# Cosine-similarity attention on one core: the TensorE warm-up reads the array of ones, and the five engine orders are replaced

## The chip, the core and the metric

The kernel runs on one core of one Trainium2 chip. A core has five engines that work side by side: TensorE (matrix multiplication, "PE" in the profile, with its weight loads as "PEld"), VectorE ("DVE"), ScalarE ("ACT"), GpSimd ("POOL") and SyncE ("SP", here only an issuer of transfers). Each runs its own list of instructions in order, and they wait for one another through semaphores. The metric is the device time of one execution in microseconds (us); shown is the median of several runs.

## The reference

For 8 batches and 12 heads, each with 512 queries, 512 keys and 64 dimensions, in float32:

```python
Q_norm = Q / (np.linalg.norm(Q, axis=-1, keepdims=True) + 1e-10)
K_norm = K / (np.linalg.norm(K, axis=-1, keepdims=True) + 1e-10)
scores = np.einsum('bhqd,bhkd->bhqk', Q_norm, K_norm) / tau
weights = np.exp(scores - np.max(scores, axis=-1, keepdims=True))
weights = weights / (np.sum(weights, axis=-1, keepdims=True) + 1e-10)
return np.einsum('bhqk,bhkd->bhqd', weights, V)
```

tau is 0.1, so the scores lie between -10 and 10.

## The kernel before

The 96 heads are worked in 48 **pairs** (s = 0 to 47). For each pair these operations exist, and the names below are the ones that the rest of the text uses:

- LD(s,0) and LD(s,1) load Q and K of a pair, LV(s) loads V (256 KB each, line 396 and 399). Pair 0 is loaded in four halves by line 393, LD(0,w,h), with w = 0 for Q, 1 for K, and h for the head. ST(s) stores the result. All but the two K halves of pair 0 and one last store are issued by SP, in the order of SP's list.
- SQ(s,...) squares Q and K. In pairs 0 to 3 it is cut in parts that ACT and POOL share (lines 329, 331, 414, 416), later it is one POOL instruction for the pair (line 422).
- SSQ(s,w) sums eight slices of the squares on TensorE (eight matmuls against the identity, line 440), and RED(s,w) on VectorE adds up what is left (line 448). Without SSQ, RED does the whole sum (line 452).
- Pairs 0 and 1 get the reciprocal root of the norm on ACT: LOG and then an exponential, NRMS for pair 0 (lines 337, 339), NEW(1,7) for pair 1 (lines 470, 473). Later groups do it on VectorE in steps NEW(g,0) to NEW(g,8) (lines 481 to 490).
- SCL(s,w) multiplies Q or K by it (lines 342, 521), on VectorE or POOL; CST(0,h) is the like for K of pair 0 (lines 316, 319).
- TR(s,w) are four transposes on TensorE (lines 351, 353, 528), and EVA(s) copies them out of PSUM on VectorE (lines 364, 536).
- SCO(s,c) and, from pair 12 on, SCG(n) are the score matmuls (lines 621, 286); EXP and EXG are the exponentials on ACT that empty the score banks (lines 626, 630, 302, 641). Pair 0 has four exponentials of 512 columns for head 0 and two of 1024 for head 1; then there are groups of 1024 and, from pair 12 on, of 1024 and 1536 columns in turn over five PSUM banks.
- VC(s) casts V on POOL (line 646). PV(s,h,i), four matmuls each (line 658), multiplies the weights with V; a column of ones in V gives the sum of the weights. RCP and NRM on VectorE divide (lines 671, 673).
- One quarter of pair 43 has its exponential on VectorE and POOL instead of ACT (steps X and Y, lines 580 to 588).

Before all this TensorE runs **warm** (line 203): eight matmuls of 512 columns whose result nobody reads. FILL(0) to FILL(9) (line 206) are single matmuls of 64 to 384 columns, also unread, that stand in between in TensorE's list. `warm` waits for the POOL instruction that makes the identity (line 193, out of the array of ones that line 192 writes) and for a VectorE memset of the array `warm_in` (line 207).

The **order** of each engine is written out by hand: `ORDER` holds, for each of the five, the numbers of the operations in the order in which they were added, and line 37 in `schedule` turns them into lists. The waits follow from the operations' needs; nothing is reordered at run time, so an instruction that waits holds up all that stand behind it on its engine, SP's transfers too. The head of the lists, in names (pairs 0 and 1 up to the first group of pair 1):

```
POOL  one eye eps vone SQ(0,1,1) SQ(0,1,0) CST(0,1) SQ(1,1,1) SQ(2,0) SQ(2,1) SQ(3,0) SQ(3,1) VC(0)
ACT   SQ(0,0,0) CST(0,0) SQ(0,0,1) LOG(0,0,0) NRMS(0,0,0) LOG(0,1,1) NRMS(0,1,1) LOG(0,0,1) LOG(0,1,0) NRMS(0,0,1)
      SQ(1,0) NRMS(0,1,0) SQ(1,1) EXP(0,1,0) EXP(0,0,0) LOG(1) NEW(1,7) EXP(0,3,0) EXP(0,2,0) EXP(0,0,1) EXP(0,2,1) EXP(1,0)
PE    warm FILL(9) FILL(4) TR(0,1,0) TR(0,0,0) FILL(3) FILL(2) FILL(0) TR(0,1,1) SCO(0,1,0) SCO(0,3,0) SCO(0,0,0) FILL(1)
      SSQ(1,0) SSQ(1,1) TR(0,0,1) SCO(0,2,0) FILL(6) FILL(5) SSQ(2,0) FILL(7) SCO(0,0,1) SCO(0,1,1) SSQ(2,1)
      TR(1,1) TR(1,0) SCO(0,3,1) SCO(0,2,1) SSQ(3,0) FILL(8) SSQ(3,1) SCO(1,0) PV(0,0,0)
DVE   wz RED(0,0,0) RED(0,1,1) RED(0,0,1) SCL(0,0,0) RED(0,1,0) EVA(0,1,0) EVA(0,0,0) EVA(0,1,1) SCL(0,0,1) RED(1,0) RED(1,1)
SP    LD(0,0,0) LD(0,0,1) LD(1,0) LD(1,1) LD(2,0) LD(2,1) LD(3,0) LD(3,1) LV(0)
```

Of the kernel before, what the change touches and what calls it, by code (L numbers as in the profile page):

```python
# [118 lines left out]
def bass_cosine_similarity_attention_kernel(  # L119
# [8 lines left out]
    BATCH, NHEAD, SEQ, DIM = Q.shape  # L128
    assert SEQ == 512 and DIM == 64 and NHEAD % 2 == 0
    NT = SEQ // 128  # L130
# [6 lines left out]
    def sb(name, shape, dt):  # L137
        return nc.alloc_sbuf_tensor(name, shape, dt)
# [14 lines left out]
    ones = sb("ones", [128, 128], bf16)  # L153
    ident = sb("ident", [128, 128], bf16)
    eps = sb("eps", [128, 1], f32)
    warm_in = sb("warm_in", [128, SEQ], bf16)
# [12 lines left out]
    P = Program(nc)  # L169
# [31 lines left out]
    def warm(e):  # L201
        for k in range(WARM):
            last = e.matmul(out=o_ps[1][:, :], lhsT=ident[:, :], rhs=warm_in[:, :], start=True, stop=True)
        return last

    P.fill = lambda e, n: e.matmul(out=o_ps[1][:, 0:n], lhsT=ident[:, :], rhs=warm_in[:, 0:n], start=True, stop=True)
    P.add("wz", "dve", "sm_dve", -100, [], lambda e: e.memset(warm_in[:, :], 0.0))
    P.add("warm", "pe", "warm", -100, ["eye", "wz"], warm)
# [566 lines left out]
def slack(s, most):  # L775
# [13 lines left out]
    ),  # L789
    "pool": (  # L790
# [6 lines left out]
    ),  # L797
    "dve": (
# [22 lines left out]
    ),  # L821
# [75 lines left out]
```

## Time and profile before

| | us |
|---|---|
| median of 3 runs | 188.52 (188.34 to 188.87) |
| the profiled execution, its own time | 188.81 |
| span of its instructions | 187.0 |
| ACT busy | 180.1 (96%) |
| PE busy | 174.6 (93%) |
| DVE busy | 169.5 (91%) |
| POOL busy | 161.8 (87%) |

The span runs from the first to the last instruction of the profiled execution; 1.8 us of its time lie outside. A row of the timeline reads: start, duration (both us), engine, line, operation, output and inputs, number of instructions merged, and in brackets the idle time before it and what ended that. A busy share says little here, since four engines are near full; what matters is which wait ends last in a stretch.

### The profile page before, as it was taken

What the parts mean: (1) busy time and instruction counts of PE and PEld (TensorE: products, weight loads), DVE (VectorE), ACT (ScalarE), POOL (GpSimd) and SP (SyncE); (2) the same over time, 40 slices, a digit from 0 to 9 for tenths busy, and PEclk for the clock granted to TensorE, in tenths of its full rate; (3) what the DMA queues carried; (4) which work ended last, traced back from release to release, by engine and by line L of the source; (5) the groups of instructions that cost most, each with busy time, mean ns of one, the idle gap of its engine ahead of it and who ended that gap; (6) DMA issues with size and microseconds to landing.
All of it is one profiled execution on the core that took longest, in us unless ns stands there. A gap on an engine that the chain in (4) does not pass through costs nothing.

```text
span 187.0 us, 6660 instructions
## 1 busy us (share of the span) xinstructions
PE 174.6 (93%) x2714; PEld 106.2 (57%) x2714; DVE 169.5 (91%) x552; ACT 180.1 (96%) x186; POOL 161.8 (87%) x150
## 2 busy tenths in 40 slices
PE   6998999999999999999999999999999899899992
PEld 2555666556665556466566565556655465455562
DVE  1799999999999999989999989899999999979663
ACT  5789999999999999999999999999999999999993
POOL 3699999999999999999999999899999796495300
PEclk9999999999999999999999999999999999999999
DMA  5999999999999999998799999994646925001537
GB/s 167 329 354 352 350 349 349 343 377 383 366 317 332 301 380 358 321 376 274 177 368 306 329 382 365 379 370 155 200 135 172 326 68 171 4 0 57 171 110 234
DMA packets 52446, 50.76 MB, mean 271 GB/s; under 512 B 3136, under 2 KB 52416, under 8 KB 52416
## 3 DMA queue, kind: packets, MB, share of 16 engines
q1 hardware_dynamic: 51984, 50.02, 81.6%
q8 instruction: 21, 0.34, 0.8%
q10 hardware_dynamic: 432, 0.33, 0.5%
q14 instruction: 9, 0.07, 0.1%
HBM read 37.75 MB, written 12.58 MB: 269 GB/s over the span
## 4 chain that ended last, share of the span: by engine, by line
ACT 92%; DMA 3%; PE 2%; DVE 1%; issue 0%; SPq 0%
ACT et L302 90%; DMA qk<-in_Q_dram 3%; DVE qn L521 1%; ACT et L630 1%; PE scps L286 1%; SPq L393 0%; ACT et L641 0%; ACT sq L414 0%; PE ops L440 0%; PE scps L621 0%; ACT ob L706 0%; DVE ob L710 0%; PE tps L528 0%; PE ops L689 0%; DVE rd L702 0%
## 5 line engine op out<-in xcount | busy, mean ns | idle before, releaser
L302 ACT ACTIVATE et<-scps 128x1024 bf16<-128x1024 f32 (+1 forms) x159 | 169.0, 1259 | 0.3 <-PE scps L286 0.2
L422 POOL TENSOR_TENSOR sq<-qk 128x1024 bf16<-128x1024 f32 x44 | 83.3, 1908 | 0.0
L286 PE MATMUL scps<-qt 64*128 64x512 bf16 x374 | 74.0, 385 | 6.7 <-ACT et L302 4.6
L658 PEld LDWEIGHTS ops<-vb,et 128*128 128x128 bf16 x1504 | 55.6, 98 | 32.1 <-issue 16.5
L658 PE MATMUL ops<-vb,et 128*128 128x65 bf16 x1504 | 72.0, 194 | 0.3 <-DVE ob L673 0.3
L521 POOL TENSOR_TENSOR qn<-qk,rk 128x512 bf16<-128x512 f32 x38 | 39.8, 1055 | 2.1 <-DVE rk L486 1.9
L673 DVE TENSOR_TENSOR ob<-ops,rd 128x256 f32<-128x256 f32 x94 | 39.0, 417 | 0.8
L528 PE MATMUL tps<-ident,qn 128*128 128x128 bf16 x376 | 33.3, 220 | 0.4 <-DVE ys L481 0.3
L536 DVE COPY qt<-tps 128x1024 bf16<-128x1024 bf16 x47 | 32.1, 682 | 1.5 <-PE tps L528 1.2
L646 POOL TENSOR_SCALAR vb<-vf 128x512 bf16<-128x512 f32 x48 | 30.2, 640 | 3.0 <-DVE et L587 3.0
L528 PEld LDWEIGHTS tps<-ident,qn 128*128 128x128 bf16 x376 | 21.6, 98 | 13.1 <-issue 7.4
L286 PEld LDWEIGHTS scps<-qt 64*128 64x128 bf16 x374 | 16.3, 93 | 22.1 <-ACT et L302 13.8
L521 DVE TENSOR_TENSOR qn<-qk,ops 128x512 bf16<-128x512 f32 x41 | 27.0, 674 | 0.0
L452 DVE TENSOR_REDUCE xn<-sq 128x8 f32<-128x512 bf16 x38 | 25.2, 674 | 0.2
L671 DVE RECIPROCAL rd<-ops 128x4 f32<-128x4 f32 x94 | 16.1, 175 | 5.0 <-PE ops L658 3.7
L440 PE MATMUL ops<-sq,ident 128*128 128x64 bf16 x384 | 19.0, 193 | 0.0
L440 PEld LDWEIGHTS ops<-sq,ident 128*128 128x128 bf16 x384 | 14.3, 98 | 3.9 <-issue 2.4
L521 DVE TENSOR_TENSOR qn<-qk,scps 128x512 bf16<-128x512 f32 x15 | 9.9, 676 | 0.1
L448 DVE TENSOR_REDUCE xn<-ops 128x8 f32<-128x64 f32 x34 | 7.0, 210 | 0.5 <-PE ops L440 0.5
L416 POOL TENSOR_TENSOR sq<-qk 128x512 bf16<-128x512 f32 (+1 forms) x5 | 4.6, 956 | 1.1 <-DMA qk<-in_K_dram 1.0
L452 DVE TENSOR_REDUCE scps<-sq 128x8 f32<-128x512 bf16 x8 | 5.4, 684 | 0.1
L587 POOL TENSOR_TENSOR xz<-xz 128x1024 f32<-128x1024 f32 x1 | 1.9, 1893 | 3.9 <-DVE xz L582 3.9
(73 smaller groups left out, 78.4 us busy)
## 6 DMA issues: line engine op xcount, KB each, us to landing
vf<-in_V_dram SPq DMA_DIRECT2D x48, 256.0 KB, 6.2
qk<-in_Q_dram SPq DMA_DIRECT2D x47, 256.0 KB, 6.4
qk<-in_K_dram SPq DMA_DIRECT2D x47, 256.0 KB, 6.2
out_dram<-ob SPq DMA_DIRECT2D x47, 256.0 KB, 4.6
qk<-in_Q_dram SPq DMA_DIRECT2D x2, 128.0 KB, 2.6
qk<-in_K_dram ACTq DMA_DIRECT2D x2, 128.0 KB, 2.9
out_dram<-ob SPq DMA_DIRECT2D x1, 128.0 KB, 2.2
out_dram<-ob SPq DMA_DIRECT2D x1, 64.0 KB, 1.9
```

The source lines that it names most:

```text
L286: last = e.matmul(out=sc_ps[:, b, :], lhsT=qt[s % R_QT][64 * h : 64 * h + 64, 1, c, :], rhs=qt[s % R_QT][64 * h : 64 * h + 64, 0, :, :], s ...
L302: lambda e: e.activation(out=et_all[:, i : i + len(us), :], in_=sc_ps[:, banks[0] : banks[0] + len(us), :], func=ACT.Exp, scale=math.log(2 ...
L422: lambda e: e.tensor_tensor(out=sqf, in0=data, in1=data, op=ALU.mult))
L440: last = e.matmul(out=o_ps[bank][:, 320:384], lhsT=ident[:, :], rhs=sq[iqs][:, 8 * w : 8 * w + 8, 8 * k : 8 * k + 8], start=(k == 0), stop ...
L452: lambda e, w=w, dst=dst: e.tensor_reduce(out=dst, in_=sq[iqs][:, 8 * w : 8 * w + 8, :], axis=AX.X, op=ALU.add))
L521: lambda e, w=w, r=r: e.tensor_tensor(out=qn[iqn][:, w].rearrange("p t h d -> p h t d"), in0=qk[iq][:, w].rearrange("p h (t d) -> p h t d" ...
L528: last = e.transpose(t_ps[:, w, t, :], qn[iqn][:, w, t].rearrange("p h d -> p (h d)"), ident[:, :])
L536: lambda e: e.tensor_copy(out=qt[iqt][:, :, :, :].rearrange("p w t x -> p (w t x)"), in_=t_ps[:, :, :, :].rearrange("p w t x -> p (w t x)")))
L646: lambda e: e.tensor_scalar(out=vb[:, iq, :, :, 0:DIM].rearrange("p c h d -> p h c d"), in0=vf[iv][:, :, :].rearrange("p h (c d) -> p h c ...
L658: last = e.matmul(out=o_ps[h][:, 65 * t : 65 * t + 65], lhsT=et[iet][:, c, h, 128 * t : 128 * t + 128], rhs=vb[:, iq, c, h, :], start=(c = ...
L671: lambda e, h=h, grid=grid: e.reciprocal(out=rd[io][:, h, :], in_=grid[:, :, DIM]))
L673: lambda e, h=h, grid=grid: e.tensor_tensor(out=ob[io][:, h], in0=grid[:, :, 0:DIM], in1=rd[io][:, h, :].unsqueeze(2).to_broadcast([128, N ...
```

## The change

The array `warm_in` and its VectorE memset go away. `warm` and the FILLs take the array of ones both as the weights and as the moving operand, which repeats its 128 columns four times (64 columns n/64 times for a FILL of n columns); `warm` now waits for the memset of the ones alone. The numbers of columns and of matmuls stay. All five orders are replaced. The operation `wz` is gone from the list, so every number above 5 stands for the operation that had one more before.

```diff
-    warm_in = sb("warm_in", [128, SEQ], bf16)
...
     def warm(e):
         for k in range(WARM):
-            last = e.matmul(out=o_ps[1][:, :], lhsT=ident[:, :], rhs=warm_in[:, :], start=True, stop=True)
+            last = e.matmul(out=o_ps[1][:, :].rearrange("p (k x) -> p k x", k=NT), lhsT=ones[:, :], rhs=ones[:, :].unsqueeze(1).to_broadcast([128, NT, 128]),
+                            start=True, stop=True)
         return last
 
-    P.fill = lambda e, n: e.matmul(out=o_ps[1][:, 0:n], lhsT=ident[:, :], rhs=warm_in[:, 0:n], start=True, stop=True)
-    P.add("wz", "dve", "sm_dve", -100, [], lambda e: e.memset(warm_in[:, :], 0.0))
-    P.add("warm", "pe", "warm", -100, ["eye", "wz"], warm)
+    P.fill = lambda e, n: e.matmul(
+        out=o_ps[1][:, 0:n].rearrange("p (k x) -> p k x", x=64), lhsT=ones[:, :],
+        rhs=ones[:, 0:64].unsqueeze(1).to_broadcast([128, n // 64, 64]), start=True, stop=True)
+    P.add("warm", "pe", "warm", -100, ["one"], warm)
...
     "sp": (
-        "7 8 68 69 107 108 152 153 11 196 197 240 239 70 109 273 316 274 154 315 198 392 349 658 350 469 393 427 502 241 "
+        "6 7 67 68 106 107 152 151 10 195 196 238 239 315 69 272 273 108 348 153 314 349 425 392 391 240 105 426 197 316 "
...
```

The head of the new lists, in names:

```
POOL  one eye eps vone SQ(0,1,0) SQ(0,1,1) CST(0,1) SQ(1,1,1) SQ(2,0) SQ(2,1) SQ(3,1) SQ(3,0) VC(0)
      SQ(4,0) SQ(5,0) VC(1) SCL(3,1) SQ(6,0) VC(3) VC(2) SCL(5,1) SQ(7,0) SQ(8,0) SQ(9,0) VC(4) SCL(6,1)
ACT   SQ(0,0,0) CST(0,0) LOG(0,0,0) SQ(0,0,1) NRMS(0,0,0) LOG(0,1,1) NRMS(0,1,1) LOG(0,0,1) NRMS(0,0,1) LOG(0,1,0)
      SQ(1,0) SQ(1,1) NRMS(0,1,0) EXP(0,0,0) LOG(1) NEW(1,7) EXP(0,3,0) EXP(0,1,0) EXP(0,2,0) EXP(0,0,1) EXP(0,2,1) EXP(1,0)
PE    warm TR(0,1,0) FILL(3) FILL(4) FILL(1) FILL(2) TR(0,0,0) TR(0,1,1) FILL(0) SCO(0,0,0) TR(0,0,1) FILL(9)
      SSQ(1,0) SSQ(1,1) SCO(0,2,0) SCO(0,3,0) SCO(0,1,0) FILL(6) FILL(5) FILL(7) SSQ(2,0) SCO(0,0,1) SCO(0,3,1) SSQ(2,1)
      SCO(0,1,1) TR(1,0) TR(1,1) SCO(0,2,1) FILL(8) SSQ(3,1) SSQ(3,0) SCO(1,0) PV(0,0,0)
DVE   RED(0,0,0) RED(0,1,1) RED(0,0,1) SCL(0,0,0) EVA(0,1,0) RED(0,1,0) EVA(0,0,0) SCL(0,0,1) EVA(0,1,1) RED(1,0) RED(1,1)
SP    LD(0,0,0) LD(0,0,1) LD(1,0) LD(1,1) LD(2,0) LD(2,1) LD(3,1) LD(3,0) LV(0) LD(4,0) LD(4,1) LD(5,0) LD(5,1) LD(7,1)
      LV(1) LD(6,0) LD(6,1) LV(2) LD(8,0) LV(3) LD(7,0) LD(8,1) LD(10,0) LD(9,1) LD(9,0) LV(5) ST(1) LD(10,1) LV(4) LV(7)
```

In the old lists POOL goes on after VC(0) with SQ(4,0) SQ(5,0) VC(1) SCL(3,1) VC(2) SQ(6,0) VC(3) SQ(7,0) SCL(5,1) VC(4) SQ(8,0) SQ(9,0) SCL(6,1), and SP has no store among its first 46 issues. TensorE has SCO(5,1) PV(4,0,0) PV(4,0,1) PV(4,0,2) SCO(5,2) in the old list and one PV(4,0,3) more ahead of SCO(5,2) in the new one. ACT's list from EXP(1,0) to its end is the same in both, and so are the last 23 entries of VectorE's.

144 rows, old and new, of the table ORDER are left out of this document.

## The prediction

> **What bounds the kernel now.** I read the page first, its span and its costliest line, the exponentials.
>
> ```profile
> span 187.0 us, 6660 instructions
> ...
> L302 ACT ACTIVATE et<-scps 128x1024 bf16<-128x1024 f32 (+1 forms) x159 | 169.0, 1259 | 0.3 <-PE scps L286 0.2
> ```
>
> Ahead of all 159 exponentials of line 302 ACT idled 0.3 us in all, and they alone take 169 us. The chain of waits in order of time says where the rest lies:
>
> ```profile
> 13.20 154.88 ACT et L302 x146
> ...
> 168.12 0.62 PE scps L286 x3
> ...
> 182.20 0.73 ACT et L641
> ```
>
> From 13.20, where EXP(1,0) starts, to 182.20 the end is set by ACT alone, but for one wait of a few tenths at 168. Its list from EXP(1,0) on is the same in both versions. So the time is **13.2 us of head, 169 us of ACT at its own pace, and a tail**. A better order can shorten the head and the tail; in the middle it can only lose. That one wait is of pair 43: a group of a single score bank covers too little for the next three, whatever the order; I leave it in.
>
> The head on ACT, from its timeline:
>
> ```profile
> 6.95 0.63 ACT L414 ACTIVATE sq<-qk 128x512 bf16<-128x512 f32 x1 [0.21 <-DMA qk<-in_Q_dram]
> 7.49 0.19 ACT L339 ACTIVATE xs<-ys 128x4 f32<-128x4 f32 x1
> 7.61 0.42 ACT L414 ACTIVATE sq<-qk 128x256 bf16<-128x256 f32 x1
> 7.93 1.25 ACT L630 ACTIVATE et<-scps,xs 128x512 bf16<-128x512 f32 x2
> 9.10 0.31 ACT L470 ACTIVATE ys<-xs,eps 128x16 f32<-128x16 f32 x1
> 9.56 1.25 ACT L630 ACTIVATE et<-scps,xs 128x512 bf16<-128x512 f32 x2
> 10.70 1.02 ACT L626 ACTIVATE et<-scps 128x1024 bf16<-128x1024 f32 x1
> 12.10 1.02 ACT L626 ACTIVATE et<-scps 128x1024 bf16<-128x1024 f32 x1 [0.38 <-PE scps L621]
> 13.20 7.44 ACT L302 ACTIVATE et<-scps 128x1024 bf16<-128x1024 f32 x8
> ```
>
> Two exponentials of 512 columns take 1.14 us from 9.56 to the start of the next, 0.57 each; one of 1024 takes 0.92 (eight in 7.44). ACT thus lost 0.48 us ahead of 12.10 and 0.18 ahead of 13.20. What holds 13.20 is not ACT, but what feeds SCO(1,0):
>
> ```profile
> 7.65 4.72 POOL L416 TENSOR_TENSOR sq<-qk 128x256 bf16<-128x256 f32 x5 [1.03 <-DMA qk<-in_K_dram]
> ```
>
> ```profile
> 12.43 0.41 PE L440 MATMUL ops<-sq,ident 128*128 128x64 bf16 x8
> 12.77 0.39 PE L286 MATMUL scps<-qt 64*128 64x512 bf16 x2
> ```
>
> **POOL's five squares** run without a gap from the landing of pair 1's K (7.6) to 12.37; the sums of the last one stand on TensorE ahead of SCO(1,0) (12.43), which starts at 12.77, ends at 13.16, and EXP(1,0) follows. So the head is set by a load and by POOL. The new orders keep this chain: POOL has the same five squares behind the same load (its last two exchanged), TensorE has both SSQ of pair 3 ahead of SCO(1,0), and SP's first six issues are the same.
>
> **The change part by part.** *The warm-up.*
>
> ```profile
> 0.78 0.20 POOL L192 MEMSET ones<- 128x128 bf16 x1 [0.29 <-POOLq L879]
> 1.06 0.29 POOL L193 TENSOR_SCALAR_AFFINE_SELECT ident<-ones 128x128 bf16<-128x128 bf16 x1
> 1.41 3.60 PE L203 MATMUL ops<-warm_in,ident 128*128 128x512 bf16 x8 [1.41 <-POOL eps L196]
> 5.31 0.64 PE L353 MATMUL ops<-ident,qn 128*64 128x128 bf16 x4
> 6.07 0.47 PE L353 MATMUL tps<-ident,qn 128*64 128x128 bf16 x4
> 6.86 0.39 PE L351 MATMUL ops<-ident,qn 128*128 128x128 bf16 x4
> 7.18 0.82 PE L621 MATMUL scps<-qt 64*128 64x512 bf16 x3
> ```
>
> The ones are there at 0.98, the identity at 1.35: the warm-up starts 0.37 us earlier, near 1.04. The removed memset frees nothing: what follows it on VectorE, RED(0,0,0), waits for ACT's first square. Its eight matmuls took 3.60 us with the last one's drain, so at most 0.45 each, or 0.88 ns a column. How fast a repeated operand is read the profile doesn't show; I take the same, and bound it by nothing below and, above, by twice (the warm-up then ends at 8.2 instead of 4.6), which would delay the first scores by over 1 us. Four transposes took 0.64 us at 5.31, 0.47 at 6.07 and 0.39 at 6.86, and three scores of 512 columns 0.82 at 7.18, where the warm-up had 0.45 for each: TensorE runs at **half clock until about 6.2**, 4.8 us after its first matmul. If the 4.8 us hold, the switch comes at 5.8. As the other end I take a half clock that lasts through the old order's first three scores, to 8.0.
>
> A rule speaks against counting on that: the Trainium skill, "TensorE: Matmul & The Clock Gate", Part 1, says the activity window (an estimate by its figure: 3.4 us) runs freely and doesn't start with the kernel, so that the same kernel has a different number of slow matmuls from run to run. By it the switch could come at any time from 4.5 to 7.9; by the one execution traced, at 5.8. One profile can't decide.
>
> *The head in its new order.* TensorE: warm to about 4.5, TR(0,1,0) (0.5 without its drain), then 1152 columns of FILL (1.0 us at half clock) to about 6.0, TR(0,0,0). That waits for SCL(0,0,0), and VectorE has the same three RED ahead of it:
>
> ```profile
> 5.61 0.41 DVE L342 TENSOR_TENSOR qn<-qk,scps 128x256 bf16<-128x256 f32 x1
> ...
> 8.84 0.22 DVE L448 TENSOR_REDUCE xs<-ops 128x8 f32<-128x64 f32 x1 [0.15 <-PE ops L440]
> ...
> 11.77 0.68 DVE L536 COPY qt<-tps 128x1024 bf16<-128x1024 bf16 x1
> ```
>
> So TR(0,0,0) starts at 6.07 as before, with its copy and TR(0,1,1) behind it SCO(0,0,0) falls near 7.2, where the old order had its first score, and is done at 7.6. On ACT both SQ now stand ahead of NRMS(0,1,0), which before filled the wait at 7.49: SQ(1,1) at 7.61, NRMS at 7.93, EXP(0,0,0) at 8.05. Cost so far 0.12.
>
> LOG(1) is next, one exponential earlier than before. It needs the second RED of pair 1, 8.84 plus 0.22, which hangs on POOL's half square (7.65 plus 0.6) and so on the load: **9.10 again**. ACT waits from 8.67 to 9.10, 0.43 us. Then come NEW(1,7) and, from 9.56 as before, three exponentials of 512 instead of two to 11.27, two of 1024 to 12.19 and 13.11. TensorE's share fits: SCO(0,1,1) needs EXP(0,1,0) done (10.13 plus 0.65) and ends at 11.23; the eight transposes of pair 1 follow to 11.77; SCO(0,2,1) ends at 12.08, before 12.19. EVA(1) moves from 11.77 to 11.80 and is done at 12.48, under the last SSQ, which POOL releases at 12.43 as before. SCO(1,0) goes at 12.77.
>
> Sum for the head: ACT alone could start EXP(1,0) at 13.11, 0.09 earlier; POOL holds it at 13.20. **Gain 0.00**, between 0.09 better and about 0.3 worse: at half clock to 8.0, SSQ(1,1) and LOG(1) come 0.3 late, and 13.11 becomes 13.41. A landing of K earlier than in this execution would gain up to 0.4 more, since LOG(1) now stands behind one exponential where two held it at 9.10.
>
> *The middle.* TensorE and ACT are both near full, and any order may break a feed. The tightest place I found is pair 4's cast of V:
>
> ```profile
> 17.22 1.05 POOL L521 TENSOR_TENSOR qn<-qk,rk 128x512 bf16<-128x512 f32 x1
> ...
> 24.13 0.64 POOL L646 TENSOR_SCALAR vb<-vf 128x512 bf16<-128x512 f32 x1
> 24.71 3.75 POOL L422 TENSOR_TENSOR sq<-qk 128x1024 bf16<-128x1024 f32 x2
> ```
>
> ```profile
> 28.35 0.54 PE L658 MATMUL ops<-vb,et 128*128 128x65 bf16 x12
> ```
>
> VC(4) stood at 24.13, 4 us early. Now SQ(8,0) and SQ(9,0) go first: from 17.22 SCL 1.0, SQ(6,0) 1.86, two casts 1.16, SCL 1.0, three SQ 5.6, so VC(4) at 27.8, done at 28.45. PV(4,0,0), at 28.35 before, starts near 28.55, with four PV (sixteen matmuls at 0.03, 0.5) ahead of SCO(5,2) instead of three: that ends near 29.5, and EXP(5,2) is due near 29.6 (18 steps of 0.91 behind EXP(1,0)). Cost 0, with 0.1 us to spare.
>
> *The tail* has the same last entries on ACT and VectorE: 0.
>
> **Sum.** The profiled execution is 187.0 of span and 1.81 around it, 188.81, 0.29 above the median of 188.52. All terms are zero, so I forecast 188.5 for the median, its own range 188.1 to 189.0 (0.4 for an earlier landing, 0.5 for 0.3 of clock and 0.2 at POOL's edge). I call same what lies within 0.3%, 0.57 us, about what a measurement of this kernel can tell from no change.
>
> **Rivals.** (1) *The clock gains.* If the typical execution before keeps half clock to 8.0 instead of 6.2, the old order suffers: FILL(3), FILL(2), FILL(0), 896 columns, cost 0.4 more (half of 0.88 ns each), the transposes 0.25 a group (0.64 less 0.39), and EXP(0,0,0) stands behind three scores at double length, so that LOG(1) comes some 0.85 later (0.4, 0.25, and 0.2 for the two scores ahead of it); the new order, with one score and few columns there, loses the 0.2 by which 13.41 passes 13.20. That is 0.6 better: 187.9. For it: the runs before spread over 0.53 us. Against it: the profiled execution has the early switch and is yet slower than the median. The skill's rule above makes such runs possible.
>
> (2) *V comes late*, the losing case. SP's new list has ST(1) as its 27th issue, ahead of LD(10,1) and LV(4).
>
> ```profile
> 15.45 4.30 SPq L396 DMA_DIRECT2D qk<-in_K_dram  x5
> ```
>
> ```profile
> 22.19 0.42 DVE L673 TENSOR_TENSOR ob<-ops,rd 128x256 f32<-128x256 f32 x1
> ```
>
> ```profile
> vf<-in_V_dram SPq DMA_DIRECT2D x48, 256.0 KB, 6.2
> ```
>
> The 27th issue falls near 18.3 (the fourth of those five), but ST(1) waits for NRM(1,1), done at 22.61: SP stands for 4.3 us, and LV(4) is issued near 23.8. With 6.2 us to landing it would be there at 30.0, VC(4) done at 30.65, PV(4,0,0) 2.1 us late, all of it a gap on ACT: 190.6. It decides from a landing after 27.8. Against it: the 6.2 us are mostly queue, seven or eight transfers at the 0.86 us of those five, and five of them are gone when SP moves again at 22.6; two or three are left, and ST(1), LD(10,1) and LV(4) follow, five at 0.86. I put its landing near 27, and 189.6 for half the delay.
>
> (3) *The warm-up does not start earlier*, since something other than the identity holds TensorE to 1.4: then the switch stays where it was, and by the sum above the time too, 188.5.
>
> **Chances.** Forecast with (3), 0.60; (1) 0.17, which is also faster by over 0.3%; (2) and the like of it 0.23, slower. The range from 187.8 to 189.7 holds the forecast, (1), and half of (2).
>
> **What would show it.** Warm-up at 1.04, its eight matmuls again in 3.6 us: first step right. LOG(1) at 9.10 behind a wait of 0.4 on VectorE, POOL's squares again from 7.65 to 12.37, EXP(1,0) at 13.20: the head right. EXP(1,0) before 12.9, or the first square of pair 1 before 7.3: head wrong. Idle time of line 302 still near 0.3: the middle right; a wait near 29.5 with POOL's cast as its cause: (2).

## The result

| | median | lowest and highest | executions |
|---|---|---|---|
| before | 188.61 us | 188.34 to 189.14 | 11 |
| after | 190.37 us | 189.09 to 193.27 | 11 |

The ratio after to before is **1.0069, 95% interval 1.0043 to 1.0095**: the changed kernel is slower. The ratios of this document leave out executions more than 1.5% above the fastest of their kernel: here four of 191.97 to 193.27 us, whose mean granted clock was 0.991 (with them the two medians stand at 1.0093), and below two of twelve with the warm-up alone (192.89 and 193.25), three of six with the old head and the new middle (192.97, 193.44, 218.23) and one of six with only ST(34) moved (215.22). The profiled execution took 189.82 us.

### The profile page after: what moved, and what is told of

Its sections match the earlier page's. It is cut to its first block, busy times and chain, and to the rows that moved or that the text cites. A ratio compares the mean times of both kernels' runs of the same rounds, so it can differ in the third digit from the quotient of the medians.

```text
span 187.8 us, 6654 instructions
## 1 busy us (share of the span) xinstructions
PE 174.7 (93%) x2714; PEld 106.1 (56%) x2714; DVE 169.6 (90%) x551; ACT 180.9 (96%) x186; POOL 161.9 (86%) x150
## 4 chain that ended last, share of the span: by engine, by line
ACT 71%; DVE 12%; DMA 7%; SPq 4%; PE 3%; POOL 1%; issue 1%; ACTq 0%; DVEq 0%
ACT et L303 69%; DMA qk<-in_Q_dram 4%; DVE qn L522 4%; SPq L397 2%; DVE qt L537 2%; DVE ob L674 2%; DMA qk<-in_K_dram 2%; DMA out_dram<-ob 2%; PE ops L659 1%; SPq L400 1%; POOL sq L423 1%; DVE scps L453 1%; SPq L678 1%; PE scps L287 1%; DVE scps L449 1%
## 5 line engine op out<-in xcount | busy, mean ns | idle before, releaser
L336 DVE TENSOR_REDUCE xs<-sq 128x4 f32<-128x256 bf16 x4 | 1.6, 412 | 4.6 <-ACT sq L330 3.7
```

## The profile after

The page of the changed kernel: the span, the exponentials (the group that stood at line 302), and POOL's squares.

```profile
span 187.8 us, 6654 instructions
...
L303 ACT ACTIVATE et<-scps 128x1024 bf16<-128x1024 f32 (+1 forms) x159 | 169.7, 1242 | 0.7 <-PE scps L287 0.5
L423 POOL TENSOR_TENSOR sq<-qk 128x1024 bf16<-128x1024 f32 x44 | 83.0, 1900 | 0.9 <-DMA qk<-in_Q_dram 0.9
```

The same squares on the page of the kernel before:

```profile
L422 POOL TENSOR_TENSOR sq<-qk 128x1024 bf16<-128x1024 f32 x44 | 83.3, 1908 | 0.0
```

Busy and idle time of the exponentials are together 170.4 us, where they were 169.3 (169.0 and 0.3): 1.1 us more. The span grew by 0.8. So the loss lies **in the middle**, between the first group of pair 1 and the end, and the head gave something back. POOL's squares now wait 0.9 us for a load of Q; before none of them waited.

The head, from three timelines of the changed kernel (TensorE, POOL, ACT):

```profile
1.04 3.47 PE L202 MATMUL ops<-ones 128*128 128x512 bf16 x8 [1.04 <-POOL ones L191]
4.44 0.41 PE L354 MATMUL ops<-ident,qn 128*64 128x128 bf16 x4
```

```profile
7.41 4.74 POOL L417 TENSOR_TENSOR sq<-qk 128x256 bf16<-128x256 f32 x5 [0.75 <-DMA qk<-in_K_dram]
```

```profile
8.89 0.31 ACT L471 ACTIVATE ys<-xs,eps 128x16 f32<-128x16 f32 x1 [0.16 <-DVE xs L449]
...
13.04 26.97 ACT L303 ACTIVATE et<-scps 128x1024 bf16<-128x1024 f32 x29
40.35 20.74 ACT L303 ACTIVATE et<-scps 128x1024 bf16<-128x1024 f32 x21 [0.34 <-PE scps L287]
```

EXP(1,0) starts at 13.04 instead of 13.20. K of pair 1 came 0.24 earlier (7.41 for 7.65), and POOL's five squares took the same 4.7 us behind it. From 13.04 ACT goes through 29 groups of exponentials; then it waits for scores, until 40.35.

The chain of waits of the changed kernel around that place, in order of time (start, duration, what):

```profile
22.06 0.35 DVE ob L674
22.43 0.38 SPq L678
22.85 0.60 SPq L397
...
28.48 0.47 SPq L678
28.99 7.15 DMA qk<-in_Q_dram
36.22 1.90 POOL sq L423
38.14 0.69 DVE scps L453
38.84 0.34 DVE ob L674
39.22 0.54 PE ops L659 x12
39.76 0.22 PE tps L529 x4
39.98 0.34 PE scps L287 x2
40.35 123.05 ACT et L303 x112
```

Read it forward: NRM(1,1) on VectorE ends at 22.41; it releases SP, which was standing at ST(1); SP then works off its list at about 0.5 us an issue and comes to LD(11,0) at 28.99; the load takes 7.15 us; SQ(11,0) on POOL waits for it until 36.22; RED(11,0), NRM(5,1), PV(6,1), a group of transposes and the scores of pair 8 follow in turn, and ACT's exponential starts late at 40.35. Nothing in this chain belongs to the warm-up. The waits of ACT beyond those of the kernel before add up to 1.27 us: 0.55 at 40 to 41.5, 0.33 near 176, 0.17 at 25.1 behind a V load issued ahead of SP's standstill (not followed further), and 0.22 in three smaller ones. Less 0.16 in the head that is 1.1, and the last exponential does end 1.1 later (184.55 for 183.47). Of the span 0.3 came back behind it: the last store, issued 1.13 behind the last exponential in both kernels, landed after 1.65 us instead of 1.96.

SP's own timeline, changed kernel:

```profile
16.45 1.07 SPq L400 DMA_DIRECT2D vf<-in_V_dram  x1
22.43 0.38 SPq L678 DMA_DIRECT2D out_dram<-ob  x1
```

After LV(5), which ends at 17.52, SP issues nothing for **4.9 us**. What that does to the transfers, from the table by windows (the length of the stretch; busy time and instructions of PE, PEld, DVE, ACT, POOL; then granted clock, share of the DMA engines, GB/s), first before, then after:

```profile
20.00:24.00 4.00, 4.00 (x69) 2.61 (x66) 4.00 (x15) 4.00 (x5) 4.00 (x4) 1.00 1.10 350
24.00:28.00 4.00, 3.80 (x71) 2.51 (x67) 3.93 (x18) 4.00 (x6) 4.00 (x4) 1.00 1.10 350
```

```profile
20.00:24.00 4.00, 3.92 (x68) 2.58 (x67) 3.97 (x13) 4.00 (x6) 3.77 (x4) 1.00 0.75 241
24.00:28.00 4.00, 3.87 (x72) 2.58 (x68) 3.98 (x17) 3.94 (x6) 4.00 (x4) 1.00 0.92 246
```

109 and 104 GB/s less over 4 us each are 0.85 MB: a little over three loads of 256 KB that have not moved by 28 us. At 350 GB/s they take 2.4 us to make up. The queue ran nearly dry while SP stood (85 GB/s from 22 to 23 us), and the missing bytes show up later as a late load.

A second store waits near the end. The chain of the changed kernel there:

```profile
169.96 0.37 SPq L678
170.38 0.47 SPq L678
170.89 3.01 DMA out_dram<-ob
173.99 0.44 DVE ob L674
174.47 0.42 PE ops L659 x8
```

NRM(42,1) at 173.99 needs the output buffer of pair 34. ST(34) is the 184th issue in the new list, behind ST(39), ST(40) and ST(38), and SP waits for the result of pair 40 (169.94) before it comes to ST(34), whose result has been there for long.

## Experiments

Three theories, and what each puts the loss on. **S**: in SP's new list stores stand ahead of loads that are needed, ST(1) in 27th place above all. **H**: the head, with the warm-up out of the ones and the early half clock. **D**: the new lists are tighter everywhere in the middle. All ratios are to the kernel before, with 95% intervals. "Waits of ACT", read in the one traced execution of each kernel, are the distances between the ends of successive exponentials beyond their own length; the kernel before has one, 0.31 us at 168.8, which every kernel here has. Lists are shown by names.

### The warm-up alone

```diff
 the changed kernel's code (ones as both operands, no warm_in, no wz)
-    the five new orders
+    the five old orders (every number above 5 one lower)
```

> The kernel before with only the warm-up and the fills changed (the array of ones, waiting for its memset alone); all five orders are the old ones. Three theories on why the changed kernel is 0.7% slower. S: the new order of SP puts stores ahead of loads that are still needed, and SP stands at them (ST(1) near 17.5 to 22.4 us, ST(34) behind ST(40) near 171 us). H: the new head or the new warm-up costs the time. D: the new orders of the middle are tighter everywhere, the stores are one place of many. S and D: same as before, 188.6 within 0.3, the wait of line 302's exponentials near 0.3 us. H, if the warm-up is at fault: 189.5 or more.

Ratio **1.0003** (0.9988 to 1.0018), median 188.84 us. The warm-up starts at 1.04, EXP(1,0) at 12.94, and ACT has no wait beyond the one it always has. By the ratio the code change costs nothing and gains nothing that can be measured. The two executions near 193 us are taken up in the last section.

### New orders in the head, old ones behind it

```diff
 the changed kernel
     the five new orders up to what starts before 13.1 us
-    the new orders behind that
+    the old orders behind that
```

> New warm-up, and each engine in its new order for what it began in the first 13.1 us of the changed kernel's profile, then in the old order for all that is left. S and D: the gain of the new head alone, EXP(1,0) at 13.0 to 13.2 and no new wait behind it, so 188.3 to 188.6. H: about as slow as the changed kernel, 189.6 to 190.

Ratio **1.0015** (0.9996 to 1.0035), median 189.17 us; EXP(1,0) at 12.93, one extra wait of 0.08 us. S and D had expected 188.3 to 188.6, H 189.6 to 190; the median lies between. H is left with at most a third of a per cent, and its interval holds no change.

### Old head, new orders behind it

```diff
 the changed kernel
-    the new orders in the head
+    the five old orders up to what starts before 13.3 us
     the new orders behind that
```

> New warm-up, each engine in its old order for what it began in the first 13.3 us of the profile of before, then in the new order. S and D: about the changed kernel's time, 189.6 to 190.2, with waits of ACT near 40 and 175 us; EXP(1,0) at 13.2. H: like before, 188.6.

Ratio **1.0064** (1.0040 to 1.0089), from three executions of 189.67 to 190.14 us: the whole loss is there without the new head. The profiled execution of this kernel can't be read for the middle, since its TensorE stayed at half clock far into the head (see the last section).

### Both stores moved back

```diff
 SP, the new list
-    LV(5) ST(1) LD(10,1) LV(4) ... LV(10) ST(2) ... ST(32) ST(39) ST(40) ST(38) ST(34) ST(41)
+    LV(5) LD(10,1) LV(4) ... LV(10) ST(1) ST(2) ... ST(32) ST(34) ST(39) ST(40) ST(38) ST(41)
```

> The changed kernel with two stores moved in SP's order: ST(1) from the 27th place to just ahead of ST(2), ST(34) from behind ST(38) to ahead of ST(39). Nothing else. S: the waits of ACT near 40 us (0.57 us) and 175 us (0.33 us) go, and with the earlier head the time is 188.5 to 189.0, the small waits near 25 and 31 us staying. D: at most half of the loss goes, 189.4 or more, with new waits elsewhere. H: no change, 189.9.

Ratio **1.0014** (0.9995 to 1.0034), median 188.90 us. Two entries of one list take the loss away, as far as the times can tell; all other new orders are still there. The small waits near 25 and 31 us, which were expected to stay, are gone too. The same windows as above:

```profile
20.00:24.00 4.00, 3.97 (x69) 2.60 (x68) 4.00 (x13) 4.00 (x6) 4.00 (x5) 1.00 1.12 352
24.00:28.00 4.00, 4.00 (x73) 2.60 (x69) 4.00 (x18) 4.00 (x6) 4.00 (x3) 1.00 1.08 345
```

The transfers run at full pace again and POOL has no gap. D falls: the new middle holds ACT without a wait as soon as SP doesn't stop.

### Only ST(1) moved back, and only ST(34)

```diff
 SP, the new list, first kernel
-    LV(5) ST(1) LD(10,1) ... LV(10) ST(2)
+    LV(5) LD(10,1) ... LV(10) ST(1) ST(2)
 SP, the new list, second kernel
-    ST(32) ST(39) ST(40) ST(38) ST(34) ST(41)
+    ST(32) ST(34) ST(39) ST(40) ST(38) ST(41)
```

> The changed kernel with ST(1) alone moved behind, to just ahead of ST(2) in SP's order; ST(34) stays where the change put it. Both moved gave 1.0014 against before, the change 1.0069. Theory S in two places: ST(1) cost the waits up to 70 us (0.9 us in the profile), ST(34) those at 175 us (0.3 us). So about 189.2, a ratio near 1.003, no wait of ACT between 20 and 70 us, and 0.3 us of waits near 175 us left.

> The changed kernel with ST(34) alone moved ahead of ST(39); ST(1) stays in the 27th place. S: the waits near 40 us (0.57 us) stay, those near 175 us go: ratio near 1.005, 189.5. If ST(34) were the whole cause: 188.9.

ST(1) alone: **1.0020** (0.9999 to 1.0042). ST(34) alone: **1.0106** (1.0065 to 1.0147), where 1.005 was expected; two executions with a clock of 0.991 count in it, and those at full clock, 189.63 to 190.36 us, lie among the changed kernel's own (189.09 to 190.93). So ST(1) is the cause that can be measured. ACT's timeline with ST(1) moved is one unbroken run of 50 groups, and POOL's with only ST(34) moved still has the wait, now twice as long:

```profile
13.29 47.22 ACT L303 ACTIVATE et<-scps 128x1024 bf16<-128x1024 f32 x50
```

```profile
36.85 1.89 POOL L423 TENSOR_TENSOR sq<-qk 128x1024 bf16<-128x1024 f32 x1 [2.04 <-DMA qk<-in_Q_dram]
```

With ST(1) moved LD(11,0) is issued at 27.40 and lands at 34.09, and POOL takes it at 35.15: a cover of 1.06 us. In the changed kernel it lands at 36.15, 2.06 later, near the 2.4 us of missing bytes; less the cover that is about POOL's wait of 0.91.

ST(34) is worth a wait of 0.2 us at 175.8 in the first kernel's trace; the times don't tell it apart from nothing.

### Another store in the same place

Is it the wait, or the store's traffic among the loads? ST(0) has the same bytes, but its result is ready 3.4 us sooner (19.00 and 22.40 in the changed kernel).

```diff
 SP, the new list (ST(34) ahead of ST(39))
-    LV(5) ST(1) LD(10,1) ... LV(8) ST(0) LD(11,0)
+    LV(5) ST(0) LD(10,1) ... LV(8) ST(1) LD(11,0)
```

> As the run with ST(34) moved, and ST(0) and ST(1) change places in SP's order: a store stands in the 27th place as before, with as many bytes, but its data are ready near 19.2 us instead of 22.4. SP stands 1.7 us instead of 4.9. If it is the wait ahead of the loads that costs (S): the transfers hardly run dry and the time falls to about 189.0, ratio 1.001 to 1.003, no wait of ACT near 40 us. If it is the store's own traffic among the loads that costs: as with ST(34) moved, near 1.005.

Ratio **1.0015** (0.9991 to 1.0039). SP's timeline:

```profile
16.59 1.07 SPq L400 DMA_DIRECT2D vf<-in_V_dram  x1
19.41 0.38 SPq L678 DMA_DIRECT2D out_dram<-ob  x1
```

SP stands for 1.75 us (17.66 to 19.41), the transfers go on from what is queued (361 and 360 GB/s from 20 to 28 us), and ACT waits nowhere else than before. A store in 27th place that SP waits 1.75 us for does no harm that can be measured; one **that SP waits 4.9 us for** does.

### The cause put into the kernel before

```diff
 SP, the old list
-    LD(8,1) LD(11,1) LD(9,1) ... LD(16,0) LD(18,0) ST(1) LV(13)
+    LD(8,1) LD(11,1) ST(1) LD(9,1) ... LD(16,0) LD(18,0) LV(13)
```

> The kernel before with one edit: ST(1) from the 47th to the 27th place in SP's order, where the change has it; warm-up, head and all other orders old. S says that the place of one store is enough for a loss: SP stands from about 18 to 22.6 us, the transfers fall to near 250 GB/s between 20 and 28 us, and waits of ACT appear between 25 and 70 us: ratio 1.002 to 1.006. If the old order has more room at its loads than the new one, the same standstill shows in the transfers but the time stays within 0.2%. D or H would have no effect at all.

Ratio **1.0155** (1.0116 to 1.0194), median 191.67 us, where 1.002 to 1.006 was expected: one number moved in the old list costs as much as the whole change, or more. (Four of its six executions had a clock of 0.981 to 0.991, and here they count; the two at full clock took 190.34 and 191.12 us.) The rate falls to 247 and 236 GB/s from 20 to 28 us, and the load that comes late is one of V:

```profile
36.66 0.63 POOL L646 TENSOR_SCALAR vb<-vf 128x512 bf16<-128x512 f32 x1 [2.00 <-DMA vf<-in_V_dram]
```

This is LV(6) for VC(6). Of the loads that POOL takes between 20 and 60 us it has the least cover in the old lists: in the trace before it lands 0.33 us before POOL takes it (34.40 and 34.73), here 2.18 later. ACT waits 1.72 us at 38.54 for it, and four times more up to 43.5, 1.27 us in all, in part for another reason (last section).

### Which load pays

The standstill fixes how many bytes are missing. Does the place of LD(11,0) in the list decide whether it hurts? S1 says one load is late and can be moved out of the way; S2 says bytes are missing and the next load takes its place.

```diff
 SP, the new list, first kernel
-    LV(5) ST(1) LD(10,1) LV(4) ... LV(8) ST(0) LD(11,0) LD(12,0)
+    LV(5) LD(11,0) ST(1) LD(10,1) LV(4) ... LV(8) ST(0) LD(12,0)
 SP, the new list, second kernel
-    LV(5) ST(1) LD(10,1) LV(4) ... LV(8) ST(0) LD(11,0) LD(12,0)
+    LV(5) ST(1) LD(11,0) LD(10,1) LV(4) ... LV(8) ST(0) LD(12,0)
```

> The changed kernel with one load moved in SP's list: LD(11,0) from 39th place, behind ST(0), to just ahead of ST(1), which still stops SP. Two readings of theory S. S1, one load is late: with LD(11,0) landed before 22, POOL's wait of 0.91 us ahead of SQ(11,0) goes, SQ(11,0) starts near 35.3 instead of 36.22, ACT's waits near 40.35 and 41.4 (0.55 us in all) go, and the ratio to the kernel before falls from 1.007 to between 1.001 and 1.004, though SP still stands from 17.5 to 22.4 and the transfers still fall to about 245 GB/s from 20 to 28 us. S2, bytes are missing: the next load in the list takes its place, ACT waits 0.4 us or more somewhere between 36 and 48, and the ratio stays at 1.005 or more.

> The changed kernel with LD(11,0) moved from 39th place in SP's list to the place right behind ST(1), so that SP stands as long as in the changed kernel and nothing more is issued before it does. S1, one load is late: LD(11,0) is issued at 22.9 instead of 28.99, lands by 27, SQ(11,0) no longer waits; LD(10,1), LV(4) and the ten issues after them come about 0.6 us later, for which VC(4) (27.96) and SQ(10,0) (31.73) have room; ACT's waits near 40.35 go, ratio between 1.001 and 1.004. S2, bytes are missing: another load is late by about as much, ACT waits 0.4 us or more between 27 and 48, ratio 1.005 or more.

With LD(11,0) ahead of the standstill: **1.0038** (1.0023 to 1.0053), median 189.35 us. POOL's wait for Q is gone, the load of V now keeps two casts 0.45 us, and ACT runs through 40 us without a wait; 0.13 at 25.3, 0.12 around 31, 0.11 at 65.7 and 0.27 at 162.3, the last also behind a late load of V, are left, and 0.18 near 176 where ST(34) stands. POOL's timeline:

```profile
30.21 1.21 POOL L647 TENSOR_SCALAR vb<-vf 128x512 bf16<-128x512 f32 x2 [0.45 <-DMA vf<-in_V_dram]
```

With LD(11,0) right behind ST(1): **1.0087** (1.0057 to 1.0116), median 190.17 us. The wait at 40 us is gone here too, but what stood between the two places came one load later, LV(4) first. POOL, TensorE and ACT of this kernel:

```profile
28.42 0.63 POOL L647 TENSOR_SCALAR vb<-vf 128x512 bf16<-128x512 f32 x1 [0.75 <-DMA vf<-in_V_dram]
```

```profile
29.19 0.64 PE L659 MATMUL ops<-vb,et 128*128 128x65 bf16 x16 [0.94 <-POOL vb L647]
```

```profile
30.20 30.79 ACT L303 ACTIVATE et<-scps 128x1024 bf16<-128x1024 f32 x32 [0.56 <-PE scps L287]
```

This is VC(4), PV(4,0,0) and EXP(5,2): the chain that the prediction's rival of the late V describes, set off by moving one load eleven places up. What S1 expected came in the first kernel, what S2 expected in the second. Both fit one reading, which is argued more than shown: bytes are missing, and the order chooses which load is late and how much cover that load has. The first kernel's interval overlaps that of the changed kernel (1.0043 to 1.0095), so that its gain rests on the traces more than on the times; and the second has 0.40 us of its waits at 162.6, behind a store and a load of V near 155, far from this standstill. None of these kernels beat the one before.

## Why the prediction was wrong

- **The warm-up: right** in its start, 1.04 as predicted, and in its eight matmuls, 3.47 us (predicted 3.6). The switch to full clock was put at 5.8, between 4.5 and 7.9. In the profiled execution the transposes at 4.44 are already fast (0.41), so it came before that; with the same warm-up, in the kernel with ST(1) moved, they were slow at 4.57 and still at 6.20:

```profile
4.57 0.63 PE L354 MATMUL ops<-ident,qn 128*64 128x128 bf16 x4
...
6.20 0.64 PE L354 MATMUL tps<-ident,qn 128*64 128x128 bf16 x4
```

  The trace's clock record puts the switch at 4.26 and at 6.93. The rule of the Trainium skill that the prediction weighed ("TensorE: Matmul & The Clock Gate", Part 1: the window runs freely) is borne out: the same start of the warm-up, switches 2.7 us apart. The lower end of 4.5, a whole window behind the start, didn't hold: 4.26 here, and 3.69 in the kernel with the new head alone. The late switch costs no more than the bound of 0.3: EXP(1,0) at 13.29, with K there as late as in the kernel before, and at 13.43 in the kernel with ST(0) first (switch at 7.07).
- **The head: right.** A gain of 0.00, between 0.09 better and 0.3 worse, and more if K lands earlier. K landed 0.24 earlier, LOG(1) waited 0.16 instead of 0.43, and EXP(1,0) started 0.16 earlier. How soon POOL gets K differs from trace to trace, from 6.75 to 7.65, with the old head too (6.93 in the kernel before with ST(1) moved), and EXP(1,0) from 12.83 to 13.43 (all but the trace of the last section). The two experiments on the head give 1.0003 and 1.0015.
- **The middle: this step failed**, "Cost 0, with 0.1 us to spare". Of its place the sum was near: VC(4) at 27.96 (predicted 27.8), and PV(4,0,0) at 28.74 (28.55). But it looked at one cast, and asked only whether its load would be there. The tightest feed was another: SQ(11,0), at 32.87 before and at 36.22 now. Where the sum has 0, ACT's waits in the middle add up to 0.94 us in the execution traced (the 1.27 less the 0.33 near 176). The half clock in mid-kernel that four executions had (last section), 2.6 us above the others on average, is no term of the sum either.
- **Rival (2), V comes late**, named the cause: ST(1) as the 27th issue, SP standing from 17.5 to 22.4 (predicted 18.3 to 22.6), the issue of LV(4) at 23.50 (predicted 23.8). Its refutation was right for LV(4) and wrong as a refutation: it followed the first loads behind the store, which find an empty queue and land soon, and stopped there (LV(4) landed 3.3 us after its issue, LD(11,0) 7.15). Every later load of the list is also behind by what the transfers lost while SP stood, 0.85 MB, and LD(11,0) was moved back in the list besides (issued at 28.99, before at 21.91). The sign that it named, a wait near 29.5, did not come. The price named, 189.6 for half the delay of the cast, is near the profiled 189.82, which came by another path: that is luck.
- **The tail: not zero**, as ST(34) now stands behind ST(40); the trace puts 0.3 us on it (0.11 and 0.22 near 176), the times nothing that can be told.
- **Rivals (1) and (3)** didn't come: with the warm-up at 1.04, the warm-up alone and the new head gave 1.0003 and 1.0015, no gain. In nine traces with that start the switch lay anywhere between 3.69 and 7.07 (a tenth is in the last section). Kernels with an earlier EXP(1,0) and next to no extra wait (12.93 and 13.01, against 13.20) are not faster than the one before, 1.0015 and 1.0014 with intervals that hold 1. But 13.20 is one execution: the old head started EXP(1,0) at 12.83 in another trace. What the typical execution before has stays open.

## What to carry to other kernels

In a list that is worked in order, a store is a wait: find out when its data is ready, and what stands behind it. When a queue stands still, don't ask only whether the next load is late; count the bytes that weren't moved, and follow them down the list to the load with the least cover. The Trainium skill ("Perfetto Trace Analysis", DMA Optimizations) suggests one issuing engine for inputs and another for outputs, above all where there are loops or control flow. No run here tried it; these show what a shared list can cost: 1.0155 for one store 20 places too early.

## What the runs showed of the hardware

**The clock comes in steps of 3.41 us, all through the kernel.** The stretches at full clock in the traces last 53 (before) and 54 (after) times 3.413 us, and in the kernel before with ST(1) moved 10 times, then one step of half clock, then 43 times. That step is, it seems, the other reason for ACT's waits there. The windows along the steps of that kernel:

```profile
32.01:35.42 3.41, 3.04 (x47) 1.72 (x44) 3.41 (x17) 3.41 (x5) 2.64 (x2) 1.00 1.09 356
35.42:38.83 3.41, 1.76 (x34) 1.28 (x33) 1.66 (x4) 1.80 (x3) 2.17 (x3) 1.00 1.10 348
38.84:42.25 3.41, 3.41 (x35) 1.82 (x32) 3.00 (x11) 2.77 (x3) 3.41 (x3) 0.50 1.12 354
42.25:45.66 3.41, 3.01 (x50) 1.84 (x48) 2.81 (x13) 3.20 (x4) 3.41 (x4) 1.00 1.07 374
```

In the step in which V was late TensorE was busy for 1.76 of 3.41 us, and in the next it got half its clock: busy throughout, it did 35 matmuls, where the step behind has 50 in 3.01 us, and ACT waited again. How much of the 1.27 us is the clock's isn't shown; with only ST(34) moved ACT also waited again, 0.60 us behind its first wait of 1.02, and there the worst step stayed at full clock:

```profile
35.39:38.80 3.41, 2.11 (x35) 1.34 (x33) 1.51 (x7) 3.27 (x4) 1.95 (x2) 1.00 1.10 370
```

So the edge lay between 1.76 and 2.11 us of 3.41 in these two executions. The ends of five other traces agree: half clock behind last steps of 1.34, 1.60 and 1.69 us, full clock behind 2.21 and 2.34. The Trainium skill ("TensorE: Matmul & The Clock Gate", HAM oscillation) warns of gaps over about 3.4 us; here 1.65 us without a matmul, in a step that was thin otherwise, were enough. One such step in 190 us is a mean clock of 0.991. A mean of 0.992 or less was seen in 4 of 11 executions of the changed kernel, 4 of 6 of the kernel before with ST(1) moved, 3 of 6 with only ST(34) moved (one of them at 0.662), 1 of 6 with the old head and the new middle (0.68) and 1 of 12 with ST(1) moved back, and in none of the 69 of the kernel before that were timed beside the experiments (0.995 and up). That the late load caused it in the changed kernel too is likely and not shown, for none of those four was traced.

**A warm-up doesn't guarantee the clock.** In the profiled execution of the kernel with the old head and the new middle, TensorE worked at half clock until 17.2 us, with the same warm-up from 1.04, and EXP(1,0) started at 17.48. The two steps from 6.94 to 13.77 were busy throughout and did not bring the switch; why stays open. The eight transposes of pair 1 took 1.04 us, 0.62 in the changed kernel.

```profile
13.84 1.04 PE L529 MATMUL tps<-ident,qn 128*128 128x128 bf16 x8
```

The column of the granted clock shows 1.00 for that stretch, so that it can be seen in the durations of the matmuls alone. This execution took 193.44 us. The two of 192.89 and 193.25 us with the warm-up alone, whose head is the same, look alike (mean clock 0.999) but were not traced; of the kernel before, with the later warm-up, none of the 69 took more than 190.16 us. So the earlier warm-up under the old head may not be free.
